# Transformer block on one core: the value phase and the attention in one hand-placed order on TensorE, ScalarE and VectorE

## The chip, the cores and the metric

The kernel runs on one core of one Trainium2 chip. The time is the device time of one execution in microseconds (us), the median of several runs; smaller is better. The changed kernel and the kernel before are compared on the same chip. The engines are named as the profile names them: PE is TensorE (matmuls and transposes; PEld is its weight load), DVE is VectorE, ACT is ScalarE, POOL is GpSimd, SP is SyncE, which here only issues DMAs.

## The reference, cut to what matters

One residual block over x of 512 rows by 2048 columns, all in float32: 8 heads of stick-breaking attention (SB) and 8 heads of forgetting attention (fox), 128 columns a head, then an MLP of width 8192.

```python
h = rmsnorm(x, g_attn)
proj = h @ w_in                                   # 2048 x 6152: q, k, v of SB, q, k, v of fox, 8 gate columns
log_f = log_sigmoid(proj[..., o1:] + b_f)         # fox gates
# SB head: z = q k^T / sqrt(128), strictly causal
a = where(causal, exp(log_sigmoid(z) + sum of log_sigmoid(-z) over the later keys), 0);  o = a @ v
# fox head: c = cumsum(log_f)
p = softmax(where(causal, z + c_i - c_j, -inf));  o = p @ v
mixed = concat(head_rmsnorm(o_sb, g_out_sb), head_rmsnorm(o_fox, g_out_fox))
x = x + mixed @ w_out
x = x + relu(rmsnorm(x, g_mlp) @ w_up) ** 2 @ w_down
y = rmsnorm(x, g_final)
```

## The kernel before, in words

**Arithmetic.** Every float32 operand of a large matmul is split into a high and a low part (`split`, lines L66 to L73: ACT casts the high part, L68, and DVE subtracts it from the source for the low part, L69). `mm3` (L100 to L103) multiplies high by high, high by low and low by high, so a product is three matmuls. `load_w` (L85) loads a piece of weights into tile `wraw` and splits it into `wh` and `wl`.

**Stages.** The program runs through five stages, one after the other on PE.

1. *Value phase*, up to about 181 us. Sixteen chunks of x are transposed (`transpose_x`), each scaled by g_attn and split into hH and hL. Each chunk is at once multiplied with the values of the first pair of heads and the 8 gate columns (264 columns; sums in the four banks `ps`, two from the pool `accs[1]`, two with tag `more` from the pool of the transposes, `trp`). Loads of x and of these weights are issued by SP in the order of the loop: x of a chunk pair where a new block begins, then the weights of the pair. `squares_of_x` sums the squares on ACT, `row_rstd` makes from them r1, the row scale of the first norm. ACT then scales the first values by r1 out of PSUM into `first_v`, DVE makes `gates` (L281), and SP stores the values in DRAM (`vd`). Two groups of six blocks of value columns follow, each as seven products of a Strassen-like scheme (`v_product`, 96 matmuls of 384 columns each; banks X and Y from `accs`, Z from `more`). DVE forms sums of weights and of x (`make_left`, x11, x21, f5, f3), ACT and DVE split them, and `saved` and `added` combine the products, scale them by r1 and store them in `vd`.
2. *Attention*, from 181 to about 669 us: 16 heads in pairs, in the order fox 6, 7, 0 to 5, then SB 0 to 7. For each head `project_q` computes q and k (`accq`, 2 x 48 matmuls of 512 columns), scales them by SCALE and by rb, which is r1 along the free axis (tile `qf`, L418), and splits them into the `u` tiles. `scores` is 12 matmuls into tile `s`. `attend_fox` or `attend_sb` makes the weights `w` from them (ACT and DVE in turn, causal masks on POOL; in SB the weights end with the subtraction L501 and an Exp). `weigh` transposes `w` (tile `pt`, 10 transposes, L450), splits it into `ph` and `pl`, multiplies it with the values (tile `o`, 12 matmuls), and does the norm of the head: square, copy and cast on ACT (L476, L477), low part on DVE, two matmuls with ones (`ssq`, L482), Ln and Exp on ACT (L483, L484), four steps on DVE that end in `mixed`.
   The values of a pair come back from `vd` (`load_v`, tile `vr`). Those of the last pair are computed here: `accumulate_v`, 192 matmuls of 256 columns, after the last projections, then `take_v`.
   Beside the heads, ACT, DVE and SP prepare stage 3 (`sums_of_weights`, L563): sums and differences of the four quadrants of w_out, with the splits of some of them (`tboth`, `thi`). For pairs 0 to 3 this is done once, whole, in the half of `mixed` that is still free. For pairs 4 to 7 it is done in two halves d = 0 and d = 1, eight in all, in a tile `ws` of one buffer: load from w_out, sums (L575), store to `wsums`; for d = 0 also two splits through the tile `tboth`, also of one buffer, with stores to `wraws`, and a split `thi`.
3. The product with w_out. 4. w_up with the square of relu. 5. w_down and the last norm. These keep their code.

**What sets the order.** Stages 3 to 5 are written as manual schedules. In stages 1 and 2 a list scheduler places the instructions of all engines by simulated times; attention work stands in `tc.high_priority()`. Tiles come from pools, and a tile that is taken again waits until its last use is over.

Of the kernel before, what the change touches and what calls it, by code (L numbers as in the profile page):

```python
# [14 lines left out]
P = 128  # L15
# [4 lines left out]
NH = 8  # L20
# [16 lines left out]
def block_kernel(ctx, tc, x, g_attn, w_in, b_f, g_out_sb, g_out_fox, w_out, g_mlp, w_up, w_down, g_final, y):  # L37
# [16 lines left out]
    acc_cms = [tc.tile_pool(name=f"acc{c}", bufs=2, space=PSUM, reuse_waits="tile") for c in "ab"]  # L54
    accs = [cm.__enter__() for cm in acc_cms]
    acc_turn = [0]

    class acc:
        @staticmethod
        def tile(*args, **kwargs):  # L60
            acc_turn[0] += 1
            return accs[1 - acc_turn[0] % 2].tile(*args, **kwargs)

# [20 lines left out]

    def load_w(src, a, b):  # L85

        raw = wp.tile([P, a, b], F32, tag="wraw", name="wraw")
        src = src if isinstance(src, list) else [src]
        for i, r in enumerate(src):
            n = b // len(src)  # L90
            sp.dma_start(raw[:, :, i * n:(i + 1) * n], r)
        out = []
        per = min(a, 2 * NT // b)
        for i in range(0, a, per):
            hi, lo = (w.rearrange("p (a b) -> p a b", a=per) for w in hi_lo(per * b))
            split(hi, lo, raw[:, i:i + per, :])
            out += [(hi[:, j, :], lo[:, j, :]) for j in range(per)]
        return out
# [22 lines left out]

    def along_free(trp, r, wide):

        for t in range(TB):
            dve.tensor_copy(wide[:, t * P:(t + 1) * P], r[:, t:t + 1].to_broadcast([P, P]))
        ps = trp.tile([P, NT], F32, tag="o", name="trb")
        for t in range(TB):
            pe.transpose(ps[:, t * P:(t + 1) * P], wide[:, t * P:(t + 1) * P], ident)
        return ps
# [42 lines left out]
    order = [NH + h for h in (6, 7, 0, 1, 2, 3, 4, 5)] + list(range(NH))  # L172

    def v_columns(h):
        return 2 * WSB + h * P if h < NH else o0 + 2 * WSB + (h - NH) * P

    with ExitStack() as stage:
        vf = stage.enter_context(tc.tile_pool(name="vf", bufs=1, reuse_waits="tile"))
        vq = [stage.enter_context(tc.tile_pool(name="vq0", bufs=1, side="right", reuse_waits="tile"))]
        trp = stage.enter_context(tc.tile_pool(name="tr0", bufs=2, space=PSUM))  # L180
        K8 = KC // 2

        def eighth(i, name, dt=F32R):
            return vf.tile([P, K8, 2 * P], dt, tag=f"e{i}", name=name)

        x11, x21, x12, f5 = (eighth(i, name, F32) for i, name in enumerate(("x11", "x21", "x12", "f5")))
# [7 lines left out]
        def banks(pool_, tag="acc"):  # L194
            return [pool_.tile([P, NT], F32, tag=tag, name="acc" + tag) for _ in range(2)]

        vrows = w_in.rearrange("(s a p) c -> s p a c", s=2, p=P)

        def quadrant(i, s, j, c0):
            t_ = vtile(i)  # L200
            for a in range(0, K8, 2):
                sp.dma_start(t_[:, a:a + 2], vrows[s][:, a:a + 2, c0 + j * NV:c0 + (j + 1) * NV])
            return t_

        with tc.tile_pool(name="xr", bufs=1, side="right", reuse_waits="tile") as xr:
            xt = [xr.tile([P, 2, TB, NT], F32, name=f"x{c}") for c in "ab"]

            def x_block(k):
                c = k // 4
                return xt[c % 2][:, c // 2]  # L210

            def load_x(k, n):
                i = k % 4
                sp.dma_start(x_block(k)[:, :, i * P:(i + n) * P], xq[:, :, k * P:(k + n) * P])

            def columns(out, v, n):
                ps = trp.tile([P, NT], F32, tag="tr", name="trg")
                pe.transpose(ps[:, :n], v, ident[:n, :n])
                dve.tensor_copy(out, ps[:, :n])

            def transpose_x(k):
                ps = trp.tile([P, NT], F32, tag="tr", name="tr")
                for t in range(TB):
                    last = pe.transpose(ps[:, t * P:(t + 1) * P], x_block(k)[:, t, k % 4 * P:(k % 4 + 1) * P], ident)
                g = g_in[:, k:k + 1]
                split(hH[k], hL[k], ps, g)
                a = k % K8
                if k < K8:
                    for half, out in enumerate((x11, x21)):
                        act.mul(out[:, a, :], ps[:, half * 2 * P:(half + 1) * 2 * P], g)  # L230
                else:
                    dve.scalar_tensor_tensor(f5[:, a, :], ps[:, 2 * P:], g, x21[:, a, :], op0=ALU.mult, op1=ALU.add)
                    dve.tensor_scalar(x12[:, a, :], ps[:, :2 * P], g, None, op0=ALU.mult)
                return last

            def squares_of_x(half, last):
                with tc.issue_after(last.ins):
                    for t in range(TB):
                        x_ = xt[half][:, :, t, :]
                        act.activation(x_, x_, AF.Square, accum_out=ss1[:, t, half:half + 1])  # L240

            Y, Z = banks(accs[1]), banks(trp, "more")
            ps = Y + Z
            LOADS = {0: 1, 1: 1, 2: 2, 4: 4}
            w_rows = w_in.rearrange("(s a p) c -> a p s c", s=2, p=P)
            c0, m = v_columns(order[0]), 2 * P + NH
            w_of = {}
            for k in range(K8):
                for j in (k, k + K8):
                    if k in LOADS:  # L250
                        load_x(j, LOADS[k])
                    if k == 0:
                        w_of[j] = load_w(w_rows[k][:, j // K8:j // K8 + 1, c0:c0 + m], 1, m)[0]
                if k == 0:
                    columns(g_in, g_rows, KC)
                else:
                    w_of[k], w_of[k + K8] = load_w(w_rows[k][:, :, c0:c0 + m], 2, m)
                for j in (k, k + K8):
                    last = transpose_x(j)
                    for t in range(TB):  # L260
                        ts = slice(t * P, (t + 1) * P)
                        mm3(ps[t][:, :m], hH[j][:, ts], hL[j][:, ts], *w_of[j], j == 0, j == KC - 1)
                if k in (3, 7):
                    squares_of_x(k // 4, last)
            b21 = quadrant(0, 1, 0, v_columns(order[2]))
            column_g = [g_mlp, g_out_sb, g_out_fox]
            v = xr.tile([KC + 2 * NH, P], F32, name="rows")
            i = 0
            for r in (g[0].rearrange("(h p) -> h p", p=P) for g in column_g):
                act.dma_start(v[i:i + r.shape[0], :], r)  # L270
                i += r.shape[0]
            columns(g_rest, v, KC + 2 * NH)
            dve.tensor_scalar(g_rest[:, KC:], g_rest[:, KC:], -0.5 / P, None, op0=ALU.mult)
            act.dma_start(bf, b_f.to_broadcast([P, NH]))
            r1 = row_rstd(ss1, "r1")
# [12 lines left out]
        for a, f in zip(HALVES, f3):  # L288
            dve.tensor_tensor(f, x12[:, a], x11[:, a], op=ALU.subtract)
# [1209 lines left out]
```

## Time and profile before

| | before |
|---|---|
| median of 3 runs | 2082.83 us (2081.82 to 2083.07) |
| the profiled execution, own time | 2082.69 us |
| its span, first to last instruction | 2081.0 us |
| PE busy | 2030.2 us (98%), 10410 matmuls |
| DVE busy | 1733.1 us (83%) |
| ACT busy | 1128.2 us (54%) |
| POOL busy | 53.1 us (3%) |
| mean granted PE clock | 0.991 |
| PE busy from 0 to 181 us | 46.65 of the first 60, 52.13 of the next 60, 60.38 of the last 61 |
| PE busy from 300 to 500 us | 195.59 of 200 |
| PE busy from 636 to 676 us | 25.01 of 40, granted clock 0.74 |

The busy share of an engine is the time in which it executes matmuls, transposes or element-wise work. The granted clock is the share of its full rate that PE was given in a stretch; where it is below 1, PE is busy but slower. The span is a little shorter than the execution's own time, which holds the start and the end of the program too.

### The profile page before, as it was taken

The page shows a single profiled execution, that of the slowest core. Times are in us where ns is not written, and L with a number is a line of the kernel's source. Part 1 is how long each engine was busy: PE and PEld are TensorE (multiplying, and loading weights), DVE is VectorE, ACT ScalarE, POOL GpSimd, SP SyncE. Part 2 cuts the span into 40 slices and gives each one's busy share as a digit, 9 for nine tenths or more (in the row PEclk, how much of TensorE's full clock was granted, in tenths as well). Part 3 has the DMA queues.
Part 4 walks back from the last instruction along what each step waited for, and adds up shares of the span by engine and source line. Part 5 has one row for each costly group of instructions (what it writes and reads, how often), then busy time and mean ns, then how long its engine had stood idle before and what let it go on. Part 6 is the DMA issues. An engine that isn't in the chain of part 4 may idle for free.

```text
span 2081.0 us, 27247 instructions
## 1 busy us (share of the span) xinstructions
PE 2030.2 (98%) x10410; PEld 1749.6 (84%) x10410; DVE 1733.1 (83%) x1979; ACT 1128.2 (54%) x1623; POOL 53.1 (3%) x73
## 2 busy tenths in 40 slices
PE   7799999999997999999999999999999999999998
PEld 7799888878886888988888888888888888888887
DVE  5875787776576667899999999999799899898896
ACT  6544444445455466667677677677644444444443
POOL 0000000000010000000000000000000000000004
PEclk9999999999998999999999999999999999999999
DMA  5345887763323885366756756667686565665642
GB/s 184 118 133 199 288 289 225 224 211 83 84 71 130 292 293 193 102 208 199 222 184 201 220 185 202 217 188 236 211 306 248 223 212 202 233 235 200 217 157 92
DMA packets 269571, 411.89 MB, mean 198 GB/s; under 512 B 10184, under 2 KB 165368, under 8 KB 262912
## 3 DMA queue, kind: packets, MB, share of 16 engines
q1 hardware_dynamic: 268480, 408.02, 59.0%
q10 hardware_dynamic: 960, 2.13, 0.3%
q8 instruction: 82, 1.34, 0.2%
q14 instruction: 49, 0.40, 0.1%
HBM read 313.62 MB, written 96.49 MB: 197 GB/s over the span
## 4 chain that ended last, share of the span: by engine, by line
PE 85%; DVE 6%; DMA 4%; ACT 2%; issue 1%; SPq 0%; POOL 0%; ACTq 0%; DVEq 0%; POOLq 0%
PE psa L733 10%; PE accd L102 8%; PE accd L103 8%; PE accd L101 8%; PE psa L735 5%; PE psc L733 5%; PE accq L103 4%; PE accq L102 4%; PE accq L101 4%; PE psc L735 3%; PE psb L733 2%; PE m L102 1%; PE m L101 1%; PE m L103 1%; PE psb L735 1%; PE accacc L101 1%
## 5 line engine op out<-in xcount | busy, mean ns | idle before, releaser
L1311 ACT CAST wh<-wd 128x1024 fp32r<-128x1024 f32 x126 | 124.9, 999 | 168.0 <-PE accd L103 54.4
L1201 DVE TENSOR_TENSOR wl<-wu,wh 128x1024 fp32r<-128x1024 f32 x157 | 191.4, 1220 | 15.3 <-ACT wh L1195 15.3
L103 PE MATMUL accq<-hH,wl 128*128 128x512 f32 x512 | 200.8, 392 | 0.0
L102 PE MATMUL accq<-hL,wh 128*128 128x512 f32 x512 | 200.8, 392 | 0.0
L101 PE MATMUL accq<-hH,wh 128*128 128x512 f32 x512 | 200.7, 392 | 0.0
L733 PE MATMUL psa<-f,wh 128*128 128x512 f32 x728 | 182.4, 393 | 0.3 <-ACT l L767 0.3
L1195 ACT CAST wh<-wu 128x1024 fp32r<-128x1024 f32 x157 | 166.4, 1060 | 28.3 <-issue 11.3
L103 PE MATMUL accd<-wh,uf 128*128 128x512 f32 x436 | 169.8, 389 | 0.0
L102 PE MATMUL accd<-wl,uf 128*128 128x512 f32 x436 | 169.8, 389 | 0.0
L101 PE MATMUL accd<-wh,uf 128*128 128x512 f32 x436 | 169.7, 389 | 0.0
L1318 DVE TENSOR_TENSOR wl<-wd,wh 128x1024 fp32r<-128x1024 f32 x126 | 144.0, 1151 | 13.2 <-ACT wh L1311 12.7
L733 PEld LDWEIGHTS psa<-f,wh 128*128 128x128 f32 x728 | 131.0, 189 | 23.9 <-ACT l L767 0.5
L1085 DVE TENSOR_TENSOR m<-m,accd 128x1024 f32<-128x1024 f32 x84 | 102.2, 1217 | 46.5 <-PE accd L103 46.5
L1311 ACT CAST wx<-wd 128x1024 fp32r<-128x1024 f32 (+1 forms) x82 | 80.8, 995 | 109.0 <-PE accd L103 42.9
L102 PEld LDWEIGHTS accq<-hL,wh 128*128 128x128 f32 x512 | 96.3, 188 | 19.3
L103 PEld LDWEIGHTS accq<-hH,wl 128*128 128x128 f32 x512 | 96.3, 188 | 19.2
L101 PEld LDWEIGHTS accq<-hH,wh 128*128 128x128 f32 x512 | 96.3, 188 | 19.2
L101 PE MATMUL accd<-wx,uf 128*128 128x512 f32 x284 | 110.6, 389 | 0.0
L102 PE MATMUL accd<-wx,uf 128*128 128x512 f32 x284 | 110.6, 389 | 0.0
L103 PE MATMUL accd<-wx,uf 128*128 128x512 f32 x284 | 110.6, 389 | 0.0
L68 ACT CAST wh<-wraw 128x1024 fp32r<-128x1024 f32 (+2 forms) x77 | 76.4, 993 | 58.2 <-PE accq L102 48.1
L735 PEld LDWEIGHTS psa<-f,wl 128*128 128x128 f32 x728 | 99.4, 191 | 7.1
(411 smaller groups left out, 5108.1 us busy)
## 6 DMA issues: line engine op xcount, KB each, us to landing
wu<-in_w_up_dram SPq DMA_DIRECT2D x60, 1024.0 KB, 6.5
ufd<-st SPq DMA_DIRECT2D x98, 512.0 KB, 4.2
wd<-in_w_down_dram SPq DMA_DIRECT2D x48, 1024.0 KB, 7.6
uf<-ufd SPq DMA_DIRECT2D x42, 1024.0 KB, 7.4
wraw<-in_w_in_dram SPq DMA_DIRECT2D x68, 512.0 KB, 4.2
wo<-wsums SPq DMA_DIRECT2D x28, 512.0 KB, 4.3
q<-in_w_in_dram SPq DMA_DIRECT2D x32, 384.0 KB, 5.3
wd<-in_w_down_dram SPq DMA_DIRECT2D x16, 768.0 KB, 6.4
```

The costliest lines, as they stand in the source:

```text
L68: ins = act.copy(hi, src)
L101: pe.matmul(out, sh, mh, start=first, stop=False, skip_group_check=True)
L102: pe.matmul(out, sh, ml, start=False, stop=False, skip_group_check=True)
L103: return pe.matmul(out, sl, mh, start=False, stop=last, skip_group_check=True)
L733: pe.matmul(ps, hi[:, a, :], f_both(p, a), start=a == PAIRS[0] and p in (1, 5), stop=False, skip_group_check=True)
L735: ins = pe.matmul(ps[:, 2 * P:], lo[:, a, :], f_parts(p, a)[0], start=False, stop=a == PAIRS[-1], skip_group_check=True)
L1085: dve.tensor_tensor(M[p][:, :, db, :], M[p][:, :, db, :], ps, op=ALU.add)
L1195: act.copy(rooms[k][0], srcs[k])
L1201: lows[0] = dve.tensor_tensor(lo, srcs.pop(k), hi.bitcast(F32), op=ALU.subtract)
L1311: act.copy(rooms[k + 3][0], srcs[k + 3])
L1318: dve.tensor_tensor(rooms[k + 2][1], srcs.pop(k + 2), rooms[k + 2][0].bitcast(F32), op=ALU.subtract)
```

## The change

Stages 1 and 2 are put into one manual schedule for PE, ACT and DVE: on these three engines the instructions stand in the order in which the program emits them. SP and POOL are still placed by the scheduler. The order of emission comes from a list of steps with planned times, `Plan`: each step is entered with a time in us, and all are emitted sorted by time. Each of the large helpers is cut into steps (load, cast, low part, multiply and so on).

- *Value phase.* The products get PSUM pools of their own (tags x, y, z with two banks each, beside the two banks of the transposes). The first values are copied out of PSUM as they are (`copy_first`) and stored; r1 is applied later, when the values of pair 0 are loaded (`high_v`, `low_v` with n = 0), and for the gates in `gates_1`. One chunk is planned at 1.95 us, one product at TP = 8.45 us. The 1 MB loads of x are planned ahead of the weight rows of the third chunk pair, and the first two pieces of q stand in SP's order by their planned times.
- *Attention.* A period of TPER = 27.05 us is planned for each head. In period n PE does, in this order: 3 projection matmuls of head n, the product of head n-2, 15 projections, the two norm matmuls of head n-2, the scores of head n-1, 66 projections, the transposes of head n-1, and the last 12 projections of head n (`marks`), so 15 projections stand between the transposes of one head and the product. The steps on ACT and DVE of the head's softmax, splits, norm and of the weight pieces have their places in the period.
- *Last pair.* Period 16 has no projection; the 192 matmuls of the last pair's values (`last_values`) lie there beside the scores and softmax of head 15. The products and norms of heads 14 and 15 follow, 2 us apart in the plan.
- *Sums of w_out.* `whole` and `half` put the steps of `sums_of_weights` into the periods: wholes begin in periods 1, 3, 5 and 7; halves (m, d) lie in periods 0 (4, 0), 1 (5, 0), 2 (4, 1), 9 (5, 1), 10 (6, 0), 11 (6, 1), 12 (7, 0) and 13 (7, 1). The tiles `ws`, `tboth` and `thi` keep one buffer.

PE's instructions are the same in kind and number.

```diff
+    class Plan:
+        def at(self, t, f, *args):
+            self.jobs.append((t, len(self.jobs), f, args))
+        def run(self):
+            for _, _, f, args in sorted(self.jobs, key=lambda j: j[:2]):
+                f(*args)
+    manual = tc.manual_schedule(engines={pe.engine, act.engine, dve.engine})
+    manual.__enter__()
...
+        vps = [stage.enter_context(tc.tile_pool(name=f"v{c}", bufs=1, space=PSUM, reuse_waits="tile")) for c in "xyz"]
...
+                plan.at(-50 + k + j / KC, load_x, j, LOADS[k])
+            plan.at(t - 3.0, turn_x, j)
+            plan.at(t - 2.5, x_high, j)
+            plan.at(t - 1.7, x_low, j)
...
+                piece = Piece(w_rows[k][:, :, c0:c0 + m], 2, m).plan(plan, -50 + k + 0.6 if k in LOADS else t - 9, t - 1.1, t - 0.95)
...
+            for dt, f in ((8.45, start), (9.75, soft), (12.4, maxed), (15.2, scan), (20.1, weights)):
+                plan.at(t + dt, f)
...
+        def half(m, d, t):
+            jobs = [(-12.0, w.load)]
+            if d == 0:
+                jobs += [(1.75, lambda: w.high(0)), (2.5, lambda: w.low(0)), (3.3, lambda: w.sum(0)), (5.4, lambda: w.high(1)),
+                         (6.7, lambda: w.low(1)), (21.5, lambda: w.sum(1)), (23.6, lambda: w.sum(2)), (23.8, w.high_6),
+                         (24.4, lambda: w.sum(3)), (25.0, w.low_6), (25.1, w.store)]
+            else:
+                jobs += [(2.5, lambda: w.sum(0)), (3.3, lambda: w.sum(1)), (6.7, lambda: w.sum(2)), (23.6, lambda: w.sum(3)), (23.7, w.store)]
...
+                    cast, low = ((-11.7, -6.9), (0.3, 5.4), (5.6, 10.9), (12.45, 13.95))[a]
+                    pieces.append(q_piece(n, which, hf).plan(plan, t + cast - 16, t + cast, t + low))
+                marks = [(0, 0, 1, 0.0), (0, 1, 6, 2.6), (0, 6, 8, 8.4), (1, 0, 8, 9.75), (2, 0, 8, 15.2), (3, 0, 4, 20.6), (3, 4, 8, 24.4)]
...
+                plan.at(t + 0.68, H.product)
+                plan.at(t + 2.7, H.square)
+                plan.at(t + 4.6, H.square_low)
+                plan.at(t + 6.0, H.norm_sums)
+                plan.at(t + 6.55, H.norm_1)
+                plan.at(t + 7.95, H.norm_2)
...
+            ts = t + 6.45 if n < 2 * NH else t + 2.95
+            plan.at(ts, H.scores)
+            tp = t + 23.3 if n < 2 * NH else t + 2.9 + 1.95 + 1.45 * 11 - 0.05
+            plan.at(tp, H.turn)
+            plan.at(tp + 1.2, H.p_high)
+            plan.at(tp + 2.5, H.p_low)
...
+                        dt = 1.45 * unit + (0 if unit < 2 else 1.95) + (0 if unit < 13 else 1.1)
+                        plan.at(t + dt, last_values, pieces, a, tt)
...
+        for m in range(4):
+            whole(m, TPER * (2 * m + 1))
+        for n, (m, d) in ((9, (5, 1)), (10, (6, 0)), (11, (6, 1)), (12, (7, 0)), (13, (7, 1)), (0, (4, 0)), (1, (5, 0)), (2, (4, 1))):
+            half(m, d, TPER * n)
+        plan.run()
+    manual.__exit__(None, None, None)
```

The functions that the changed steps call (`split`, `mm3`, the masks, the arithmetic of the norm) are as before.

More of the change, by code (lines that the diff above doesn't have):

```diff
@@ new lines, in gates_3, with gates_4 @@
+        def gates_3():
+            cps = now["cps"] = atp.tile([P, TB, 2 * NH], F32, tag="o", name="cps")
+            for t in range(TB):
+                for i in range(t + 1):
+                    pe.matmul(cps[:, t, :], utri if i == t else onesr, lf[:, i, :], start=(t == 0 and i == 0),
+                              stop=(i == t), skip_group_check=True)
+        def gates_4():
+            act.copy(cq, now["cps"][:, :, :NH])
+            dve.tensor_tensor(cq, cq, now["cps"][:, :, NH:], op=ALU.add)
@@ new lines, in last_values @@
+        def last_values(pieces, step, t):
+            if step == 0 and t == 0:
+                banks = [accs[1].tile([P, NT], F32, tag="acc", name="accv") for _ in range(2)]
+                now["v"] = [banks[t_ // 2][:, t_ % 2 * 2 * P:(t_ % 2 + 1) * 2 * P] for t_ in range(TB)]
+            ts = slice(t * P, (t + 1) * P)
+            for i in range(4):
+                k = 4 * step + i
+                mm3(now["v"][t], hH[k][:, ts], hL[k][:, ts], pieces[step].hi[:, i, :], pieces[step].lo[:, i, :],
+                    k == 0 and t % 2 == 0, k == KC - 1)
```

921 lines of the change are left out of this document (544 added, 377 removed).

## The prediction

> **What bounds the kernel now.** I read the page first, then the table of busy times by stage, then the chain and the waits of those stages in which TensorE (PE) falls short.
>
> ```profile
> span 2081.0 us, 27247 instructions
> PE 2030.2 (98%) x10410; PEld 1749.6 (84%) x10410; DVE 1733.1 (83%) x1979; ACT 1128.2 (54%) x1623; POOL 53.1 (3%) x73
> 0.00:7.00 7.00, 2.14 (x10) 1.69 (x10) 1.45 (x4) 2.80 (x4) 0.73 (x7) 1.00 0.66 188
> 7.00:27.00 20.00, 17.30 (x123) 16.32 (x121) 10.06 (x18) 13.61 (x27) 0.00 (x0) 1.00 0.92 320
> 0.00:60.00 60.00, 46.65 (x306) 43.08 (x306) 36.58 (x59) 38.84 (x70) 0.73 (x7) 0.97 0.58 192
> 60.00:120.00 60.00, 52.13 (x278) 50.65 (x279) 48.02 (x60) 28.92 (x41) 0.00 (x0) 0.91 0.38 132
> 120.00:180.00 60.00, 59.38 (x343) 59.05 (x342) 44.41 (x52) 28.64 (x37) 0.00 (x0) 1.00 0.20 67
> 300.00:400.00 100.00, 98.39 (x467) 81.44 (x465) 75.84 (x126) 46.00 (x84) 3.41 (x6) 1.00 0.75 238
> 400.00:500.00 100.00, 97.19 (x465) 80.52 (x464) 73.47 (x100) 48.90 (x66) 5.41 (x10) 1.00 0.58 174
> 636.00:648.00 12.00, 8.25 (x54) 7.15 (x53) 11.88 (x19) 7.68 (x12) 0.91 (x2) 0.92 0.62 222
> 648.00:660.00 12.00, 7.51 (x25) 5.87 (x25) 6.90 (x10) 6.07 (x8) 1.15 (x2) 0.64 0.26 87
> 660.00:669.00 9.00, 2.25 (x11) 2.25 (x12) 6.83 (x9) 2.48 (x4) 1.69 (x2) 0.50 0.01 2
> 669.00:676.00 7.00, 7.00 (x34) 5.92 (x34) 1.60 (x2) 2.82 (x4) 0.00 (x0) 0.93 0.37 120
> ```
>
> A row gives the stretch in us, its length, then busy us of PE, its weight loads, VectorE (DVE), ScalarE (ACT) and GpSimd (POOL), the granted PE clock, the DMA share and GB/s. PE is the bound. The change leaves its 10,410 instructions as they are, by kind and count, and only orders them anew, so all that can be won is PE time that is idle or at a lower clock before about 676 us. In the value phase (to 180) that is 13.35 + 7.87 + 0.62 = 21.8 us idle, and at the clock 0.03 x 46.65 + 0.09 x 52.13 = 6.1, together 27.9. In the two heads at the end (636 to 676) it is 3.75 + 4.49 + 6.75 = 15.0 idle and 0.08 x 8.25 + 0.36 x 7.51 + 0.5 x 2.25 + 0.07 x 7 = 5.0 at the clock, together 20. In the middle there is next to nothing: 1.6 + 2.8 = 4.4 in 200 us. Some 52 us are the ceiling of the gain.
>
> **Part 1, the value phase.** The longest wait that goes:
>
> ```profile
> PE accacc L101 <- DVE gates L281: 7.7, 1, 7.7
> 7.14 1.35 SPq L91 DMA_DIRECT2D wraw<-in_w_in_dram  x2
> 12.42 0.58 SPq L91 DMA_DIRECT2D wraw<-in_w_in_dram  x1
> wraw<-in_w_in_dram SPq DMA_DIRECT2D x7, 264.0 KB, 7.0
> ```
>
> Before, PE stands still until the first values are scaled by r1 and leave PSUM. The changed kernel gives the products banks of their own, copies the first values unscaled, and scales them later, when they are loaded. These later scalings (four ACT and four DVE steps for pair 0) replace one cast and one subtraction, and lie in period 1, counted below. The 7.7 us go, and with them most of the lowered clock. What stays of the 27.9: the start (7 - 2.1 = 4.9, the same loads first); a slow clock on the first matmuls, about 2; one new wait. In SyncE's (SP) order the weight rows of the third chunk pair now stand behind both 1 MB loads of x and two pieces of q. Before they were issued at 7.14; the place they get is about that of 12.42, and 7.0 to land makes 19.4. A chunk is 16 PE instructions, 17.30 / 123 x 16 = 2.25 us with the slow start in it, so PE wants the third pair, its fifth chunk, at 7 + 4 x 2.25 = 16: a wait of about 3. Further about 2 for ACT, which gets the squares of x into the last four chunk pairs, and 2 for the first group of products, where the forms of x come on top of DVE's share. Left: 4.9 + 2 + 3 + 2 + 2 = 14; gain 14 of 27.9. Bounds: 8 (DVE is as full as before in the first group) to 20 (only start and slow clock are left).
>
> **Part 2, the last pair.** Before, the last two heads' chains follow each other with nothing left to put beside them. After, the 192 value matmuls of the last pair lie beside the scores and softmax of head 15, and both products and norms follow together. Of the 20 us I leave 4: the split of the last values, and the one chain of two norms. Gain 16, bounds 11 to 18. Stage w_out then asks for its weights some 16 us sooner after the last projection; for that I put 2 back (bounds 0 and 16, the second if its loads keep their old distance from the projections).
>
> **Part 3, one period per head.** Per period PE has 96 projection matmuls, scores, transposes, product and two norm matmuls, in one fixed order: transposes, 15 projections, product, 15, norm sums, scores, 66, transposes. The softmax of a stick-breaking head must fit beside the 66.
>
> ```profile
> 591.12 0.40 PE L101 MATMUL accq<-hH,wh 128*128 128x512 f32 x1
> 596.12 0.39 PE L102 MATMUL accq<-hL,wh 128*128 128x512 f32 x1
> 651.75 1.25 ACT w L493
> 654.29 0.48 ACT n L476
> 654.77 0.47 ACT os L477
> 662.08 1.50 DVE w L501
> 666.75 2.39 PE pt L450 x10
> ```
>
> The first two rows are 22 steps apart: 5.00 / 22 = 0.227 us a matmul, so 66 take 15.0 and 15 take 3.4. The chain from the scores to the transposes took 666.75 - 651.75 = 15.0, with 0.95 of another head's work in it: 14.05. It fits with 0.9 to spare, where ACT and DVE come on time. So an undisturbed period loses nothing, and I put 3 for all of them against the 4.4 of before (-1). But ACT and DVE now stand in the plan's order, and the plan puts steps there that wait for transfers:
>
> ```profile
> wsums<-ws SPq DMA_DIRECT2D x8, 1024.0 KB, 5.2
> ws<-in_w_out_dram SPq DMA_DIRECT2D x14, 512.0 KB, 4.0
> wraws<-tboth SPq DMA_DIRECT2D x8, 512.0 KB, 4.8
> 317.49 5.95 DMA wsums<-ws
> 323.46 4.03 DMA ws<-in_w_out_dram
> 327.61 0.69 DVE ws L575
> L68 ACT CAST tboth<-ws 128x512 fp32r<-128x512 f32 x8 | 5.0, 622 | 23.1 <-DMA ws<-in_w_out_dram 14.9 <-DMA wraws<-tboth 8.2
> DVE ws L575 <- DMA ws<-in_w_out_dram: 13.1, 4, 7.4
> L69 DVE TENSOR_TENSOR pl<-ph,pl 128x512 fp32r<-128x512 f32 x14 | 9.9, 706 | 3.3 <-ACT pl L68 3.3
> L483 ACT ACTIVATE ra<-ssq,eps 128x512 f32<-128x512 f32 x15 | 10.3, 684 | 19.5 <-PE ssq L482 19.5
> L484 ACT ACTIVATE ra<-ra 128x512 f32<-128x512 f32 x15 | 9.4, 626 | 0.2
> L69 DVE TENSOR_TENSOR wl<-wraw,wh 128x1024 fp32r<-128x1024 f32 x67 | 81.9, 1222 | 10.7 <-ACT wh L68 10.6
> L68 ACT CAST wh<-wraw 128x1024 fp32r<-128x1024 f32 x67 | 70.2, 1047 | 53.5 <-PE accq L102 48.1 <-issue 2.7 <-DMA wraw<-in_w_in_dram 1.7
> L69 DVE TENSOR_TENSOR ul<-qf,uh 128x512 fp32r<-128x512 f32 x32 | 22.4, 699 | 2.4 <-ACT uh L68 2.4
> L418 DVE TENSOR_TENSOR qf<-accq,rb 128x512 f32<-128x512 f32 x16 | 10.9, 683 | 11.0 <-PE accq L103 10.9
> ```
>
> The half sums of w_out (tile ws) have one buffer in both kernels, and eight of them come in periods 0, 1, 2 and 9 to 13. The next half's load waits for the store of the last: 5.2 + 4.0 and some 0.4 between them, 9.6 from DVE's last step on one half to the first on the next (the chain: 317.49 to 327.61 is 10.1). The plan leaves some 4.5: the last step at 23.6 to 25.0 of a period, the next half's first at 1.75 (d = 0, ACT) or 2.5 (d = 1, DVE) of the following 27.05.
>
> Zero is the end of a period's scores; a period is 27.05 in the plan. Transposes end at 16.2 (15.0 and half of 2.39, which ran at half clock), the product runs from 19.6 to 21.5, the norm sums could start at 24.9. The squares need 0.48 + 0.47 + 0.62 on ACT and 0.71 on DVE, so undisturbed they are ready at 23.8 and the second norm matmul goes at 25.1. DVE ends the subtraction of the weights (L501) at 14.05 - (666.75 - 663.58) = 10.9, with a weight piece put before the scan some 11.2; then come 1.22 + 0.68 + 0.70, to 13.8, and the half's last steps of 0.69.
> - Periods 11 and 13 (d = 1). The half before has four steps left there: 16.6. First data at 26.2, the second transfer some 1.2 later (its issue takes half of the pair's time on SP, and it shares the engines; an estimate). Both sums stand ahead of the square's low part on DVE: 27.4 + 0.69 + 0.71 = 28.8. The second norm matmul goes at 28.9 instead of 25.1, and behind it on PE are the scores: 3.8 each.
> - Periods 10 and 12 (d = 0). The half before has one step left: 14.5, data at 24.1. ACT's cast tboth stands ahead of the squares: 24.7, squares 26.3, low part 27.0: 2.0 late, so scores end at 29.1 instead of 27.1. Then the second cast needs the one buffer of tboth back: DVE's low part at 25.4, 4.8 + 0.3 to store, 31.1 with the cast; a weight piece (1.05), Ln and Exp of the norm (0.68 + 0.63), and only then the softmax: 33.5 instead of 29.2, less the spare 0.9: 3.4. Together 5.4 each.
> - Periods 1 and 2: the same two waits, and period 2 has four sums of a whole besides; its end of 1 already has nine DVE steps ahead of the weights' low part. The same walk gives 4 in period 1, and in period 2 some 3 before the product and 8 before the norm sums: 15.
>
> Sum of the stalls 2 x 3.8 + 2 x 5.4 + 15 = 33.4. Below nothing they cannot go, since the PE order is fixed; the low end is half, if periods 1 and 2 are served early; the high end is 50, with wraws at 7 instead of 4.8 and the transfers of periods 0 to 2 crowded.
>
> Clock: the stall of 7.7 went with a mean of 0.91 in its 60 us, 4.7 lost. Of the six places I take four that are long enough, 1 us each: 4. The Trainium skill, TensorE: Matmul & The Clock Gate, Part 1, says that PE falls to half rate after an idle window of about 3.4 us and comes back after a busy one as long, which would be 1.7 us for each of six: 10 instead of 4, and a sum of 2097. The row of 660 to 669 shows the half rate (0.50).
>
> **Sum**, against the profiled execution's own time of 2082.69 (1.7 around its span; the median of the runs is 2082.83): -14 - 16 + 2 - 1 + 33.4 + 4 = +8.4: 2091.1, to the median 2091.2. A measurement tells some 0.2%, 4.2 us, from no change.
>
> **Rivals.**
> - Absorbed (faster). The same waits stand in the trace before (ACT 23.1, DVE 13.1 in a few stalls up to 7.4), and PE lost only 4.4 in those 200 us. If slack that I don't see takes them again, the sum is -29 and the time 2054; with half of the stalls (17) and 2 of clock it is 2073. It decides at 29 us of stalls and clock together: below that the change gains. Against it: in the order of before, 27 projections and more stood between a product and its norm matmuls, now 15, and nothing else is ready for PE. Chance 0.31, 0.10 of it for all absorbed.
> - About even: stalls of 25 and 4 for the clock give 2083. Chance 0.13.
> - A slip in every period: spare 0.9 is eaten by semaphores and DVE's queue, 1 us in 16 periods, and the first value group is bound by DVE (gain 8): 2091 + 16 + 6 = 2113. Chance 0.13.
> - Not passed on: the end of attention comes sooner, but w_out waits for its weights (16 for the 2 of part 2): 2105. Chance 0.05.
>
> **Numbers.** Forecast 2091 with 0.38. Faster by over 0.2% is the absorbed case, 0.31; within 0.2% 0.13; slower is the rest, 0.56. For 8 in 10 the low end reaches half way into full absorption, 2060; the high end takes in the slip with the stalls at their size here, 2114. The forecast's own range, with 6 either way on the value phase, 9 on the stalls and 4 on the tail, is 2080 to 2103.
>
> **What would show it.** Value phase: first projection at about 167 us instead of 181, no wait on gates, one of some 3 us before 25 us. Attention: PE waits for pl (square's low part) in periods 1, 2 and 10 to 13, each with ACT tboth or DVE ws waiting for the ws load; in the other periods, 27.2 us without a wait. Tail: one dip instead of two. It is wrong if PE waits on those steps for less than 20 us in all, or if many small waits stand before the transposes.

## The result and the profile after

The changed kernel takes 2089.87 us (median of 9 runs, 2086.89 to 2090.73) against 2082.83 (9 runs, 2080.84 to 2085.22) of the kernel before on the same chip: ratio 1.0031, interval 1.0020 to 1.0041. The forecast was 2091, some 8 us slower; it is 7 us slower. The sum came out nearly right, its terms less so: one gain was half of what I gave it, another larger, and the stalls lie partly in another place.

The page and the stages of the changed kernel (columns as in the prediction: busy us of PE, its weight loads, DVE, ACT and POOL, then the granted PE clock, DMA share and GB/s):

```profile
span 2087.8 us, 27172 instructions
PE 2034.7 (97%) x10410; PEld 1751.9 (84%) x10410; DVE 1736.5 (83%) x1966; ACT 1130.5 (54%) x1618; POOL 65.3 (3%) x73
0.00:60.00 60.00, 48.65 (x315) 45.02 (x316) 32.57 (x58) 36.75 (x65) 0.73 (x7) 0.97 0.54 178
60.00:120.00 60.00, 54.87 (x307) 52.61 (x306) 53.79 (x54) 31.79 (x41) 0.00 (x0) 1.00 0.53 181
181.00:300.00 119.00, 107.52 (x477) 89.24 (x478) 76.72 (x129) 45.69 (x82) 7.48 (x6) 0.91 0.73 237
300.00:400.00 100.00, 100.00 (x486) 84.64 (x485) 76.19 (x116) 48.22 (x84) 11.49 (x8) 1.00 0.65 202
400.00:500.00 100.00, 96.61 (x468) 80.62 (x466) 76.30 (x100) 50.48 (x69) 8.16 (x10) 1.00 0.54 168
500.00:600.00 100.00, 90.71 (x422) 75.83 (x423) 70.83 (x84) 50.17 (x57) 7.81 (x12) 0.97 0.47 140
600.00:676.00 76.00, 74.63 (x446) 66.49 (x445) 48.73 (x55) 37.88 (x45) 7.48 (x12) 1.00 0.41 128
```

The end of attention is as good as full: 74.63 of 76 at full clock. So is the stretch from 300 to 400, in which heads run without half sums of w_out. The value phase still has holes (11.35 us in the first 60, 5.13 in the next), and PE stands still 11.5 us between 181 and 300, and 12.7 between 400 and 600, where before it stood still for 0 and 2.8.

What PE waited for between 181 and 700 us (waits: us in total, times, longest):

```profile
PE ssq L752 <- DVE pl L746: 13.3, 5, 5.0
PE trb L531 <- DVE rw L526: 3.8, 1, 3.8
PE pt L702 <- POOL w L620: 2.3, 2, 1.2
PE ssq L751 <- ACT pl L743: 2.1, 2, 1.1
PE o L76 <- ACT ph L711: 2.1, 1, 2.1
PE accoa L77 <- DMA wl<-wraws: 1.4, 1, 1.4
PE cps L550 <- DVE lf L59: 1.2, 1, 1.2
PE o L77 <- DVE pl L714: 1.0, 1, 1.0
```

Half of it stands at the second norm matmul (ssq, L752), which waits for the low part of the square (pl, L746), as the prediction said. The timeline of period 11 (head 9's norm) shows why: DVE stood still for the load of tile ws, did two sums, and only then the low part.

```profile
499.63 0.69 DVE L789 TENSOR_TENSOR ws<-ws 128x512 f32<-128x512 f32 x1 [4.61 <-DMA ws<-in_w_out_dram]
501.32 0.69 DVE L789 TENSOR_TENSOR ws<-ws 128x512 f32<-128x512 f32 x1 [1.00 <-DMA ws<-in_w_out_dram]
501.93 0.68 DVE L746 TENSOR_TENSOR pl<-ph,pl 128x512 fp32r<-128x512 f32 x1
502.67 0.79 PE L752 MATMUL ssq<-pl,onesr 128*128 128x512 f32 x1 [3.71 <-DVE pl L746]
566.23 0.50 PE L752 MATMUL ssq<-pl,onesr 128*128 128x512 f32 x1 [4.08 <-DVE pl L746]
```

The last row is the same matmul in period 13. Both waits, 3.71 and 4.08, stand against the forecast of 3.8 each.

A second view is used below: the start of each head's ten transposes on the timeline. Two rows of heads without a half beside them are 27.19 apart (267.98 and 295.17), so 27.2 is what a period costs when nothing is late.

```profile
228.09 0.60 PE L702 MATMUL pt<-ident,w 128*128 128x128 f32 x4
267.98 0.71 PE L702 MATMUL pt<-ident,w 128*128 128x128 f32 x5
295.17 0.60 PE L702 MATMUL pt<-ident,w 128*128 128x128 f32 x4
```

us between starts, by kernel, from the timelines (the experiments are explained below; "start" is from the first projection to the first transposes, which lie in period 1; periods 3 to 7, left out, stand at 27.2 in all of these but for period 3 of e1, 27.7, and of e5, 28.7):

| | start | period 2 | 8 | 9 | 10 | 11 | 12 | 13 | 14 | 15 |
|---|---|---|---|---|---|---|---|---|---|---|
| the change | 54.3 | 39.9 | 27.2 | 27.2 | 30.3 | 32.7 | 30.4 | 33.2 | 27.2 | 27.2 |
| e1 two ws | 58.5 | 31.9 | 27.2 | 27.2 | 30.2 | 28.9 | 31.0 | 27.2 | 27.2 | 27.2 |
| e2 moved | 45.0 | 27.2 | 32.1 | 35.5 | 30.7 | 33.1 | 31.3 | 33.3 | 30.4 | 32.3 |
| e3 moved, late | 45.0 | 27.2 | 27.2 | 30.2 | 27.2 | 27.2 | 27.2 | 27.2 | 27.2 | 27.2 |
| e5 late only | 46.4 | 38.6 | 27.2 | 27.2 | 27.2 | 27.2 | 27.2 | 27.2 | 27.2 | 27.2 |
| e6 other order | 45.0 | 27.2 | 27.2 | 28.5 | 27.2 | 27.2 | 27.3 | 27.2 | 27.3 | 27.2 |

### The profile page after: what moved, and what is told of

It is laid out like the page before. It is cut to its first block, busy times and chain, and to the rows that moved or that the text cites. A ratio compares the mean times of both kernels' runs of the same rounds, so it can differ in the third digit from the quotient of the medians.

```text
span 2087.8 us, 27172 instructions
## 1 busy us (share of the span) xinstructions
PE 2034.7 (97%) x10410; PEld 1751.9 (84%) x10410; DVE 1736.5 (83%) x1966; ACT 1130.5 (54%) x1618; POOL 65.3 (3%) x73
## 4 chain that ended last, share of the span: by engine, by line
PE 83%; DVE 7%; DMA 5%; ACT 3%; issue 2%; SPq 1%; POOL 0%; ACTq 0%; DVEq 0%; POOLq 0%
PE psa L1043 10%; PE accd L77 8%; PE accd L78 8%; PE accd L76 8%; PE psa L1045 5%; PE psc L1043 5%; PE accq L76 4%; PE accq L78 4%; PE accq L77 4%; PE psc L1045 3%; PE psb L1043 2%; DMA ws<-in_w_out_dram 2%; DMA wsums<-ws 1%; PE m L77 1%; PE m L76 1%
## 5 line engine op out<-in xcount | busy, mean ns | idle before, releaser
L1628 DVE TENSOR_TENSOR wl<-wd,wh 128x1024 fp32r<-128x1024 f32 x126 | 143.9, 1151 | 13.2 <-ACT wh L1621 12.7
L76 PEld LDWEIGHTS accq<-hH,wh 128*128 128x128 f32 x512 | 97.8, 191 | 18.8
L168 ACT CAST wh<-wraw 128x1024 fp32r<-128x1024 f32 (+2 forms) x77 | 76.6, 997 | 61.9 <-PE accq L77 57.2
```

Of the source, the lines that this page charges most:

```text
L76: pe.matmul(out, sh, mh, start=first, stop=False, skip_group_check=True)
L168: act.copy(self.hi, self.source())
L1628: dve.tensor_tensor(rooms[k + 2][1], srcs.pop(k + 2), rooms[k + 2][0].bitcast(F32), op=ALU.subtract)
```

## The experiments

Ratios are to the kernel before, run beside each group of kernels on the same chip.

### e1: a second buffer for the half sums

```diff
-            w = WeightSums(m, (d,), lambda: at.tile([P, 2, 1280], F32, tag="ws", name="ws") ...
+            half_turn[0] += 1
+            if half_turn[0] % 2:
+                w = WeightSums(m, (d,), lambda: at.tile([P, 4, NT], F32, tag="ws2", name="ws"))
+            else:
+                w = ...                      # as before, tag "ws"
```

> The changed kernel with a second buffer for the half sums of w_out (tile ws), the room taken from two tiles of the last head; the order on PE, ACT and DVE is untouched. Theory (the stalls are waits for the one buffer): the d = 1 stalls of periods 11 and 13 go (11.5 us with their slow clock), of the d = 0 stalls of periods 10 and 12 (6.3) some 2 stay, since the second cast still waits for the one buffer of tboth; of the 12.7 lost in period 2 some 9 go; the 9.8 lost in period 0 stay, because the first half has no buffer before it. Together -24: 2066. Rival (the halves' steps are too many for ACT and DVE in these periods, whatever they wait for): within 4 us of 2090.

Measured 2075.72 (2074.16 to 2076.55), ratio 0.9956 (0.9941 to 0.9971): 14 us faster than the change, not 24. In stages 1 and 2 the order on the three engines is the same to the instruction, so the buffer alone was worth 14; the rival (nothing) has fallen. The d = 1 stalls have gone as expected: no ssq stands among PE's waits, and period 13 is at 27.2; the 1.7 us that period 11 is still over are what 3.4 us at half clock cost, behind a wait in period 10. Period 2 got 8 back, the start lost 4 more (ACT's second cast of the first half waited 7.87 us for the store of tboth, where it had waited 5.37). The d = 0 stalls are as long as they were, and the waits show what is left of them, the store of tboth:

```profile
ACT tboth L782 <- DMA wraws<-tboth: 10.1, 2, 5.5
PE pt L702 <- POOL w L620: 4.7, 2, 2.3
467.68 0.62 ACT L782 CAST tboth<-ws 128x512 fp32r<-128x512 f32 x1 [4.65 <-DMA wraws<-tboth]
469.16 0.68 ACT L756 ACTIVATE ra<-ssq,eps 128x512 f32<-128x512 f32 x1
470.41 1.22 ACT L642 ACTIVATE w<-s 128x1280 f32<-128x1280 f32 x1
```

ACT stands 4.65 us for the one buffer of tboth, behind it come a weight piece, the norm's Ln and Exp, and only then the softmax (L642), so the transposes are 2.3 late. That chain stands in the prediction (3.4 each); in e1's expectation I had taken it for 1.

### e2 and e3: the halves in periods 8 to 15, first as they were, then late

```diff
-        for n, (m, d) in ((9, (5, 1)), (10, (6, 0)), (11, (6, 1)), (12, (7, 0)), (13, (7, 1)), (0, (4, 0)), (1, (5, 0)), (2, (4, 1))):
-            half(m, d, TPER * n)
+        for n in range(8, 16):
+            half(n // 2, n % 2, TPER * n)
```

e3 has this too, and in `half`:

```diff
-                jobs += [(1.75, lambda: w.high(0)), (2.5, lambda: w.low(0)), (3.3, lambda: w.sum(0)), (5.4, lambda: w.high(1)),
-                         (6.7, lambda: w.low(1)), (21.5, lambda: w.sum(1)), (23.6, lambda: w.sum(2)), (23.8, w.high_6),
-                         (24.4, lambda: w.sum(3)), (25.0, w.low_6), (25.1, w.store)]
+                jobs += [(13.0, lambda: w.high(0)), (14.2, lambda: w.low(0)), (18.6, lambda: w.sum(0)), (20.9, lambda: w.high(1)),
+                         (21.45, lambda: w.low(1)), (21.5, lambda: w.sum(1)), (23.6, lambda: w.sum(2)), (TPER + 2.5, lambda: w.sum(3)),
+                         (TPER + 2.6, w.high_6), (TPER + 3.3, w.low_6), (TPER + 3.4, w.store)]
             else:
-                jobs += [(2.5, lambda: w.sum(0)), (3.3, lambda: w.sum(1)), (6.7, lambda: w.sum(2)), (23.6, lambda: w.sum(3)), (23.7, w.store)]
+                jobs += [(18.6, lambda: w.sum(0)), (21.5, lambda: w.sum(1)), (23.6, lambda: w.sum(2)), (24.4, lambda: w.sum(3)), (24.5, w.store)]
```

> The eight halves moved into periods 8 to 15, d = 0 and d = 1 in turn, each with the steps and times in its period that the changed kernel has, one buffer. Theory: periods 0 to 2 lose nothing any more (-22.5, some 2 stay), and each half that follows another costs what it cost before, 3.15 us where it is d = 0 (periods 10, 12, 14) and 5.75 where it is d = 1 (9, 11, 13, 15): 32.5 instead of 17.8. Sum -6: 2084. Rival (the loss at the start of attention is not the halves' but that of the gates and the crowded transfers after the value phase): it stays, and 2105 comes out.

> As the kernel with the halves in periods 8 to 15, and in addition the half's steps late in its period: the first step that needs the load at 13.0 (d = 0, ACT) or 18.6 (d = 1, DVE) instead of 1.75 and 2.5, the second cast of tboth 8 us behind the first, the last three steps of d = 0 early in the next period. The work is the same, one buffer. Theory (a load that is wanted 10 us after the last step on the half before finds its time): no wait on ws or tboth, every period near 27.2: 2090 - 22 - 16 = 2052. Rival (too much work for the places): a stall before the transposes in most of the periods 8 to 15, 2085 or more.

e2: 2090.46 (2085.81 to 2092.83), ratio 1.0027 (1.0017 to 1.0037). e3: 2051.97 (2051.74 to 2052.66), ratio 0.9844 (0.9827 to 0.9860). With the halves gone from periods 0 to 2, these lose nothing any more (45.0 and 27.2 in the table, instead of 54.3 and 39.9): what was lost at the start of attention belongs to the halves, and the rival with the gates has fallen. In e2, periods 10 to 15 cost 3.2 to 6.1 us each, near what they cost in the change; but period 8 is 4.9 over, where I had it free, and period 9 is 8.3 over instead of 5.75; the last whole sum has steps in both. Hence 2090 and not 2084. In e3 the same halves with the same work in the same periods and one buffer cost 3.0 us in all. Its stretch from 181 to 600 us, and PE's two longest waits between 181 and 700:

```profile
181.00:600.00 419.00, 416.83 (x2015) 351.49 (x2014) 321.48 (x441) 212.03 (x305) 41.04 (x42) 1.00 0.62 194
PE accoa L77 <- DMA wl<-wraws: 1.5, 1, 1.5
PE o L77 <- DVE pl L714: 1.3, 1, 1.3
```

It was when the steps stood in the period, not their number.

### e5: the late steps in the old periods

The second diff of e3 without the first.

> The changed kernel with the eight halves in their old periods (0, 1, 2 and 9 to 13) and only their steps late in the period, as in the kernel of 2052. This parts time from place. Theory: in periods 9 to 13 nothing waits any more (-17.8, 1 to 3 stay in period 9); in period 0 the first load, which cannot start before attention's tiles are free and landed 6 us into the period, is wanted at 13 and comes in time, so most of the 9.8 goes; in period 2 the half and the whole both want tboth and VectorE, and 5 of 12.7 stay. 2090 - 32 = 2058. Rival (the start of attention is crowded whatever the halves' times are, and only their leaving helped): 2090 - 16 = 2074.

Measured 2063.28 (2062.91 to 2063.62), ratio 0.9889 (0.9874 to 0.9904). Periods 10 to 13 are at 27.2, and the start loses 1.4 instead of 9.3. But period 2 still loses 11.4, where I had 5. There ACT's cast of the whole sum's part stands 7.58 us for the one buffer of tboth, and head 0's cast of its weights (ph, L711) behind it:

```profile
227.41 0.62 ACT L781 CAST tboth<-mixed 128x512 fp32r<-128x512 f32 x1 [7.58 <-DMA wraws<-tboth]
228.46 1.22 ACT L711 CAST ph<-pt 128x1280 fp32r<-128x1280 f32 x1
229.72 0.80 PE L76 MATMUL o<-ph,vh 128*128 128x512 f32 x1 [4.54 <-ACT ph L711]
```

So time settles periods 9 to 13 and most of the start, and place settles period 2, where a whole and halves share tboth.

### e4: GpSimd takes sums from VectorE in the value phase

```diff
-            dve.tensor_tensor(out[:, a], u[:, a], v[:, a], op=ALU.subtract)
+            (dve if a == HALVES[0] else pool).tensor_tensor(out[:, a], u[:, a], v[:, a], op=ALU.subtract)
...
-                dve.tensor_tensor(out, u, v, op=ALU.subtract)
+                (pool if self.p == 7 and self.group == 1 else dve).tensor_tensor(out, u, v, op=ALU.subtract)
...
-            dve.tensor_tensor(f, x12[:, a], x11[:, a], op=ALU.subtract)
+            pool.tensor_tensor(f, x12[:, a], x11[:, a], op=ALU.subtract)
```

and the weights of the first pair, from the fourth chunk pair on, are split 2.1 (cast) and 1.25 us (low part) earlier in the plan. The steps given to GpSimd in product 7 and f3 are entered earlier too.

> The changed kernel with its attention untouched and VectorE relieved in the value phase: the sums of product 7 in the first group, two sums of x and the difference f3 go to GpSimd (8.2 us less for VectorE between 56 and 106 us of the trace), and the weights of the first pair are split a little earlier than the chunk's x from the fourth chunk pair on. Theory (VectorE, full in the first group, makes PE wait for wl; in the first pair the low part stands behind one that waits for ACT): 4 to 5 of the 7.3 us lost in the first group and 2 to 3 of the 0.5 us waits in each chunk pair come back, first projection at 167 instead of 173.8, 2083. Rival 1 (the order of the plan, not the load of VectorE, makes the waits): 0 to -2. Rival 2 (GpSimd, which took 1.45 us for 128x512 elsewhere, is late or slows VectorE): slower than 2090.

Measured 2098.39 (2097.08 to 2098.83), ratio 1.0065 (1.0050 to 1.0080): 8 us slower than the change, the second rival. Most of it lies in the first group of products, six of which took 64.5 us instead of 57.2. Steps of DVE that lie beside GpSimd's take several times as long:

```profile
53.26 3.19 POOL L320 TENSOR_TENSOR x<-f,x 128x1024 f32<-128x1024 f32 x1
54.12 6.21 DVE L171 TENSOR_TENSOR wl<-q,wh 128x768 fp32r<-128x768 f32 x2
56.53 2.99 POOL L394 TENSOR_TENSOR f<-x,x 128x1024 f32<-128x1024 f32 x1
74.65 4.12 POOL L353 TENSOR_TENSOR q<-q,q 128x1536 f32<-128x1536 f32 x1 [4.96 <-DVE q L353]
```

In the change two such low parts take 1.82 together; here they took 6.21, and ended when two steps of GpSimd had gone by, which fits two engines that run by turns. GpSimd's steps are the slower ones (4.12 us for 128x1536, against 1.75 on DVE). The Trainium skill, SBUF — State Buffer, section Terms, says the same: the two engines share a pair of ports, one instruction holds it to its end, and the other engine blocks. Of the two edits only the earlier split won something: the second half of the first pair took 17.3 us instead of 18.4.

### e7 and e10: what the first group of products waits for

e7 is e3 with the value phase reordered and nothing on GpSimd:

```diff
-        plan.at(TV + 9.5, sums_of_x, 6, HALVES[1])
-        plan.at(TV + 8.4, sums_of_x, 7, HALVES[1])
+        plan.at(TV + 4.6, sums_of_x, 6, HALVES[1])
+        plan.at(TV + 3.0, sums_of_x, 7, HALVES[1])
...
-                piece = Piece(w_rows[k][:, :, c0:c0 + m], 2, m).plan(plan, -50 + k + 0.6 if k in LOADS else t - 9, t - 1.1, t - 0.95)
+                piece = Piece(w_rows[k][:, :, c0:c0 + m], 2, m)
+                piece.room = (vf, "e3") if k == 2 else (wp, "wraw")
+                piece.plan(plan, -48.1 if k == 2 else -50 + k + 0.6 if k in LOADS else t - 9,
+                             *((t - 3.2, t - 2.2) if k > 2 else (t - 1.1, t - 0.95)))
```

e10 is e3 without the eight sums of weights in the first group:

```diff
-                if len(w.names) > 1 and a % 4 == 0:
+                if len(w.names) > 1 and a % 4 == 0 and group == 2:
```

> The kernel of 2052 with the value phase only reordered, nothing on GpSimd: the second halves of the sums x11 and x21 go where VectorE waits for ACT behind the first pair (2.4 us out of the full stretch), the weights of the first pair from the fourth chunk pair on are split earlier, and the weights of the third pair get a place of their own in SBUF and are issued ahead of the large loads of x. Theory: the wait of 2.5 before the fifth chunk and its slow clock go (-3), the split gives 1, and of the 5.1 of waits for wl in the first group 2 go: 2046. Rival (VectorE's share of the first group sets its end): the waits move by the same sum, and 2048 or 2049 come from the other two edits.

> The kernel of 2052 without the eight sums of weights in the first group of products (14 us less for VectorE, the products then use one quadrant instead of a difference; everything else as it is). It asks what bounds PE between 50 and 107 us, where 54.5 us of the two-product blocks' time in the kernel of 2052 stand for 49.9 in the second group. Theory (VectorE is full there): the waits for wl go and each pair of products takes 16.6 to 17, 2052 - 6 = 2046. Rival (it is the order on VectorE and ScalarE, or ScalarE's casts, whatever the load): less than 2 us come back.

e7: 2047.09 (2046.77 to 2047.86), ratio 0.9812 (0.9798 to 0.9827), 4.9 below e3; in the traces the first projection comes at 168.5 instead of 173.2. The wait of 2.5 before the fifth chunk is gone with the slow clock behind it, and the first pair takes 38.3 us instead of 41.5. The first group got 1 us shorter, where I had 2 and the rival nothing, and the time lies between my 2046 and the rival's 2048.

e10: 2045.76 (2044.51 to 2046.05), ratio 0.9812 (0.9796 to 0.9829), 6.2 below e3. Six products, two at a time, take 17.7, 16.7 and 16.7 us, where e3 has 19.4, 19.0 and 18.8 (57.2 in all; the 54.5 in the expectation was wrong). In the second group two products take 16.64 in both. (A product is 48 matmuls in these traces and in the code of the kernel before, not the 96 named above.) From 66 to 86 us, first the change, then e10:

```profile
66.00:86.00 20.00, 17.66 (x98) 16.38 (x96) 19.96 (x20) 9.54 (x12) 0.00 (x0) 1.00 0.12 48
66.00:86.00 20.00, 20.00 (x117) 20.00 (x116) 13.93 (x16) 11.24 (x15) 0.00 (x0) 1.00 0.34 119
```

DVE is busy 19.96 of 20 in the change and PE 17.66; with 6 us less on DVE, PE is full. DVE's load bounds the first group, and e7's new order gave back 1 us of it.

### e8: the cover of the last softmax undone

```diff
-                ts = t + 6.45 if n < 2 * NH else t + 2.95
+                ts = t + 6.45 if n < 2 * NH else t + 25.0
-                tp = t + 23.3 if n < 2 * NH else t + 2.9 + 1.95 + 1.45 * 11 - 0.05
+                tp = t + 23.3 if n < 2 * NH else t + 41.85
-        for i, dt in ((2 * NH - 2, 1.0), (2 * NH - 1, 3.0)):
+        for i, dt in ((2 * NH - 2, 1.0), (2 * NH - 1, 19.0)):
```

> The kernel of 2052 with the cover of the last head's softmax undone: in period 16 PE computes all values of the last pair first and the scores of head 15 after them; head 14's product and norm lie beside the softmax, head 15's product follows its transposes. Theory (the last pair's values hide the chain of 14 us): PE stands still 10 to 12 us before the last transposes, some of it beside w_out's first products, and runs 3 to 5 at a lower clock: 2052 + 14 = 2066. Rival (w_out's first products, which do not need the last heads, or its weights set the end): within 4 us of 2052.

Measured 2068.40 (2068.31 to 2069.74), ratio 0.9916 (0.9899 to 0.9932): 16.4 more than e3. PE stands 11.20 us before the last transposes, which then run at the lower clock:

```profile
640.00:652.00 12.00, 0.65 (x2) 0.20 (x2) 8.12 (x12) 2.99 (x4) 2.10 (x4) 0.52 0.00 1
651.98 2.40 PE L702 MATMUL pt<-ident,w 128*128 128x128 f32 x10 [11.20 <-POOL w L620]
```

So the last pair's values beside head 15's softmax are worth 16 us, 2 more than the expectation had, and w_out passes them on: its rival has fallen.

### e6 and e9: the fastest version

e6 is e3 with the halves in the order (4,1), (4,0), (5,1), (5,0), (6,1), (6,0), (7,0), (7,1); e9 is e6 with the value phase of e7.

> The kernel of 2052 with the halves of periods 8 to 15 in another order: (4,1), (4,0), (5,1), (5,0), (6,1), (6,0), (7,0), (7,1), so that the first half to follow the last whole sum is one without splits, which needs no tboth. Theory (the 3.0 us that period 9 is over 27.2 come from the whole's and the half's steps meeting on ACT and tboth): 2 to 3 come back, and about 1 is lost in period 14, where a d = 0 half follows another: 2050.5. Rival (VectorE is too full in period 9 in any order): 2052 or 2053.

> The two edits that won on the kernel of 2052 together: the value phase reordered (2047.1) and the other order of the halves (-0.9). Theory: they lie in different stages and add up, 2046. Rival (the earlier end of the value phase meets other transfers): 2047 to 2048.

e6: 2051.11 (2051.01 to 2052.32), ratio 0.9832 (0.9818 to 0.9847). Its times overlap those of e3; the table shows period 9 at 28.5 instead of 30.2, and no loss in 14. e9: 2045.42 (2045.34 to 2045.66), ratio 0.9813 (0.9798 to 0.9827), 39 us below the kernel before beside it (2084.53) and 44 below the change. It is the lowest time. Its ratio is no better than e7's, which ran on another chip, so the gain over e7 rests on the traces: e9 has the early first projection of e7 (168.0) and the shorter period 9 of e6 (28.5 against 30.2).

```profile
span 2043.9 us, 27171 instructions
PE 2019.3 (99%) x10410; PEld 1742.3 (85%) x10410; DVE 1736.2 (85%) x1966; ACT 1130.8 (55%) x1618; POOL 67.6 (3%) x73
```

## Why the prediction was right in its sum, and where its terms were not

| term | predicted | measured |
|---|---|---|
| value phase (first projection 181.0, now 173.8) | -14 | -7.2 |
| the end of attention, with w_out | -14 | -18.6 |
| periods without a wait | -1 | about -4 |
| waits on ws and tboth in attention | +33.4 | +25.8 |
| clock in these places | +4 | +11.8 |
| sum | +8.4 | +7.8 by these rows, +6.8 by the spans |

The 25.8 are the rows of the waits above without that of accoa, which belongs to the end. The two sums differ by 1 us, which none of these rows explains. That the forecast came within 1.3 us of the measured time is in part luck: a gain in the value phase put 7 too high stands against one at the end put 5 too low, and stalls 8 too high against a clock 8 too low.

**Value phase: the term mis-sized.** The wait on gates did go, and the new wait before the fifth chunk came (2.58 against 3). What failed is "2 for the first group of products, where the forms of x come on top of DVE's share": the six products took 7.3 us more than the same in the second group, and e10 shows that this is DVE's load. The low bound I gave ("DVE is as full as before", gain 8) names the cause, and the gain of 7.2 lies just below it. The row of 60 to 120 before, 48.02 of 60 busy on DVE beside a PE that stood still for 7.7, pointed to it: take PE's stall away, and the same work has to fit in less time.

**The end.** PE lost 1.4 us from 600 to 676 (one wait of accoa), where before it lost 20: 18.6, just above the upper bound of 18. One dip instead of two was right, and it is a wait at full clock. The 4 left for the split and the norms were not needed, since w_out's first products (accoa, from 662.6 on) lie beside them; the 1.4 are w_out's own wait for its weights, for which I had put 2 back.

**Periods 10 to 13.** The d = 1 stalls were forecast at 3.8 each and came at 3.71 and 4.08, by the very steps of the walk. The d = 0 stalls were over-sized: 0.99 + 1.15 and 1.15 + 1.16 instead of 2.0 + 3.4. In these, DVE's and ACT's places were right, but both waits were shorter.

**Periods 0 to 2: the right sum in the wrong place.** The 15 of the prediction are 4 in period 1 and 11 in period 2, with nothing for period 0. PE's waits there come to 13.1: 5.0 in period 0 (trb and cps), none in period 1, 8.1 in period 2. With the low clock behind them the start lost 9.3 (54.3 against 45.0) and period 2 lost 12.7. The failing step is that period 0 was put at nothing without a reason, as if the first half could start freely because no half comes before it. But in SP's order its load (L777) and the weight piece before it waited until the last values had been stored (vd<-s), so it was issued only at 173.9:

```profile
SPq L161 <- DMA vd<-s: 3.7, 1, 3.7
SPq L777 <- DMA vd<-s: 1.1, 1, 1.1
173.91 2.19 SPq L777 DMA_DIRECT2D ws<-in_w_out_dram  x2
179.79 0.62 ACT L781 CAST tboth<-ws 128x512 fp32r<-128x512 f32 x1 [6.84 <-DMA ws<-in_w_out_dram]
182.91 0.63 DVE L526 COPY rw<-r1v 128x128 f32<-128x128 f32 x4
183.18 1.11 PE L531 MATMUL trb<-ident,rw 128*128 128x128 f32 x4 [3.76 <-DVE rw L526]
```

r1 along the free axis (rw, trb) stands behind the half's steps on DVE, and PE waits for it.

**Clock.** The waits cost more through the clock than I took. The rows below are the six stretches of attention at half clock, and last a stretch with a wait and no low clock. PE was busy 23.6 us in the six; half of that, 11.8 us, is what the low clock took, 1.6 to 2.7 each, where I had four times 1.

```profile
181.68:188.51 6.83, 5.33 (x15) 4.36 (x16) 2.99 (x11) 1.10 (x2) 0.00 (x0) 0.50 1.07 410
191.92:195.33 3.41, 3.41 (x10) 2.64 (x9) 1.16 (x2) 0.00 (x0) 0.00 (x0) 0.50 0.73 229
236.29:239.70 3.41, 3.31 (x12) 3.11 (x13) 1.94 (x4) 1.14 (x2) 0.00 (x0) 0.50 0.92 356
246.53:253.36 6.83, 4.85 (x15) 4.37 (x16) 6.76 (x9) 1.32 (x2) 0.00 (x0) 0.50 0.40 115
502.53:505.94 3.41, 3.27 (x10) 2.88 (x11) 2.85 (x5) 1.32 (x2) 0.00 (x0) 0.50 0.26 50
567.38:570.79 3.41, 3.41 (x14) 3.12 (x13) 3.06 (x5) 1.81 (x3) 0.00 (x0) 0.50 0.61 154
466.00:474.00 8.00, 6.79 (x33) 5.25 (x32) 3.91 (x5) 4.74 (x8) 0.00 (x0) 1.00 0.62 211
```

Every wait of 3.7 us or more had a lower clock in it or right behind it. So had the two waits of 2.1 and 1.0 us close together (third row), and a wait of 1.2 before the short matmuls of the gates (second row), but not the single wait of 1 us in period 10 (last row). The length of a wait does not settle it alone: in e1, two waits of 2.33 us stand before transposes at 485 and 545 us, and the clock was 0.83 from 483 to 493 but 1.00 from 543 to 553. What decides between them is not shown. The rule of the Trainium skill weighed in the prediction would have given 10 and was nearer than my 4, though the idle 3.4 us that it names did not occur before the second and third row.

**The rivals.** Absorbed waits, which had the largest chance after the forecast, did not happen: e3, which is without them, is 38 us below the change. A slip in every period did not happen either (27.2 in each undisturbed one), but the other half of that rival did: the first value group is bound by DVE. That w_out would not pass the gain on did not come true (its wait is 1.4), and an even result lies outside the interval (1.0020 to 1.0041).

## What to carry to other kernels

When a scheduler's order is replaced by a fixed one, every step that waits for a transfer stops whatever stands behind it on its engine; count from the last use of the buffer through its store and the next load, and put the first step that wants it after that time. Here the same change with eight such steps some 11 to 16 us later in their period, and in periods where, but for one, nothing else wants the buffers, turns from 7 us slower to 32 faster (ratios 1.0031 and 0.9844). A stall that goes gives back only what the next engine in that stage has to spare: look at the busy share of the others in that window first.

## What the runs showed of the hardware

That GpSimd's element-wise steps slow VectorE's by more than they take over was not expected in this size: in e4, 20 us of work on GpSimd made 8 us of loss out of an expected gain of 7, and DVE's busy time from 50 to 107 us rose from 50.30 to 52.06 although 8.2 us of its work had gone. The low clock after a wait came also after two waits of 2.1 and 1.0 us close together, which I had not counted, and after one of two waits of 2.33 us in e1. A stretch at half clock took 1.6 to 2.7 us from PE in the change, on top of the wait.
